# Gate products of the recurrent layer as one fp32 matmul on unsplit tiles, with a new transfer queue, smaller margins and scattered durations in the planner that sets the order

## The chip, the cores and the metric

The kernel runs on 1 core of one Trainium2 chip. The metric is the device time of one execution in microseconds (us). Three runs of the kernel before gave 1911.36, 1911.61 and 1918.54 us; their median is 1911.61 us. Engines are named as the profile names them: PE (matrix products), PEld (its weight loads), DVE, ACT, POOL, and SP, whose queue issues every transfer of this kernel.

## The reference

Two layers work on x, 2048 rows (frames) by 1024 columns. Each computes x = x + gate * Mixer(RMSNorm(x) * (1 + scale) + shift), where shift, scale and gate are one row each, a product of SiLU(c) with `ada_w`. A last RMSNorm follows. Everything is fp32.

```python
# layer 1: RG-LRU
proj = h @ in_w                                   # 1024 -> 2048: xb and zg
xf = causal_dwconv(xb, conv_w) + conv_b           # 4 taps
pre = einsum('bsni,knij->kbsnj', xf_by_block, gate_w) + gate_b   # 2 gates, 8 blocks of 128 x 128
r, i = sigmoid(pre)
log_a = -8 * r * softplus(-lam); a = exp(log_a)
b = sqrt(1 - exp(2 * log_a)) * (i * xf)
y = scan(h_t = a_t h_{t-1} + b_t) * silu(zg)
out = y @ out_w
# layer 2: gated DeltaNet, 8 heads of 128
q, k, v = silu(causal_dwconv(h @ in_w[:, :3072], conv_w)); z, a, b = the rest of h @ in_w
o = chunk_gated_delta_rule(l2norm(q), l2norm(k), v, decay(a), sigmoid(b))
out = (rmsnorm(o) * onorm_g * silu(z)) @ out_w
```

The product that the change rewrites is `pre`: for each of the 8 blocks of 128 columns, two 128x128 gate matrices times `xf`.

## The kernel before

**Tiles and stages.** The 2048 frames are cut into two halves u of 1024, each into two chunks i of 512. Activations lie with the columns on the partitions, so a tile is 128x512 fp32. Layer 1's input projection (`in1`) makes, for each u, n (0 to 7) and i, an x tile and a z tile; then the convolution, the gates and the scan follow in `conv1_thread` and `gates_thread`, and the result `tz` is stored to a DRAM tensor `y_d`. Layer 1's output projection (`out1_jobs`) goes through 16 blocks of 128 frames: `y_thread` loads a block from `y_d` into `yf` (one buffer, 512 KB), splits it into `yh` and `yl`, and two jobs multiply it with the weights. While it runs, the result goes to DRAM (`x_d`), comes back for the second layer's norm, is turned by 32x32 transposes that pass through DRAM (`xt_d<-xb`), and comes back as `xk` (`reload_thread`), of which `split_thread` makes the operands of layer 2's projection (`in2`). Layer 2's heads (keys, inverses, recurrence over 128-frame chunks) run between the products of `in2`; a z tile of layer 2 passes ACT (`zgate_thread`, L1042) and is stored to `z_d`. The last stage is layer 2's output projection.

**Split products.** The large products take both operands as two fp32r tiles, a rounded part and the rest, and add three products: high by high, high by low, low by high (`products`, L696; fp32r is a 4-byte type; the trace has one record for each such matmul). The gates did the same. This is the head of `gates_thread` before (L819 to L841), where `gh`, `gl` are the split gate weights that `lru_thread` makes once for each u and n (ACT `gh` L902, POOL `gl` L905):

```python
yield "act", 0.521
xh = tile_([P, TC], "xh", "xh", F32R)
act.copy(xh, xf)                                            # L828
yield "dve2", 0.599
xl = tile_([P, TC], "xr", "xl", F32R)
dve.tensor_tensor(xl, xf, f(xh), ALU.subtract)              # L831
for g in range(2):
    ctok = yield slots["c"]
    yield "pe", 0.696
    pg = ps.tile([P, TC], F32, tag="c", name="pg")
    for q, (a, b) in enumerate(((gh, xh), (gh, xl), (gl, xh))):
        pe.matmul(pg, lhsT=a[:, g, :], rhs=b, start=(q == 0), stop=(q == 2))   # L837
```

There are 2 x 8 x 2 = 32 such threads, so 64 gate products of three matmuls.

**What sets the order.** Every engine works through its instructions in the order in which they stand in the program, and one that waits holds back all behind it on that engine; SP's queue is one of these. The order is made before the run by `Weave`, a planner: each thread is a Python generator that yields what it needs next (an engine and a duration, a transfer, a buffer of a tag from `slots`, an event), and the planner keeps a clock for each engine and always lets the thread go on whose step can start first; the instruction is written there. So a number in a `yield` decides where an instruction stands, not how long it takes. `MARGIN` (2.4) is time that the planner adds behind certain transfers: all of it behind the loads of `vn` and `pq`, half of it before the cast of a layer 2 weight panel (`whi<-raw`), behind the load of `ec`, behind the stores of `hf` tiles, and behind some POOL steps. `transfer` says when the planner thinks that a transfer has landed:

```python
LANDS = {"sp": 1.375, "st": 1.07}        # loads, stores
self.free["sp"] = t + 0.45
self.free["dma"] = max(t + 1.04, self.free["dma"]) + dur
self.landed.append(self.free["dma"] + LANDS[kind])
th.t = self.landed[-1] + 0.05 if wait else t + 0.45
```

Of the kernel before, what the change touches and what calls it, by code (L numbers as in the profile page):

```python
# [9 lines left out]
F32R = mybir.dt.float32r  # L10
# [22 lines left out]
MARGIN = 2.4  # L33
# [5 lines left out]
WEIGHTS = 0.12  # L39
TABLE = 1.28  # L40
LANDS = {"sp": 1.375, "st": 1.07}
# [32 lines left out]
class Weave:  # L74
    def __init__(self):
        self.free = dict.fromkeys(("pe", "act", "dve", "pool", "sp", "dma"), 0.0)
        self.held = {"dve2": [], "pool2": []}
        self.table = "exp"
        self.landed = [0.0] * 8
        self.threads = []  # L80
        self.now = 0.0
# [19 lines left out]
    def start(self, th):  # L101
# [9 lines left out]
        if w[0] in LANDS:  # L111
            return max(th.t, self.free["sp"], self.landed[-8])
# [17 lines left out]
    def transfer(self, th, t, kind, dur, wait=True):  # L130

        self.free["sp"] = t + 0.45
        self.free["dma"] = max(t + 1.04, self.free["dma"]) + dur
        self.landed.append(self.free["dma"] + LANDS[kind])
        th.t = self.landed[-1] + 0.05 if wait else t + 0.45

    def run(self):
        while self.threads:
# [15 lines left out]
            elif w[0] in LANDS:  # L154
# [9 lines left out]
def trunk_kernel(ctx, tc, x, head, small, ada_w, ada_b, final_g, w1, gate_w, ow1, w2, wab, ow2, out):  # L164
# [64 lines left out]
    tags |= {t: ("l1", n) for t, n in {"xh": 2, "xf1": 2, "tg": 4, "th": 2, "tz": 2, "gw": 1, "gh": 1, "gl": 1, "head": 1}.items()}  # L229
# [79 lines left out]
    def first_loads_thread():  # L309

        yield ev("firstpanel")
        for half in range(2):
# [5 lines left out]
            for q in range(4):  # L318
                for n in (2 * half, 2 * half + 1):
                    part, d = FIRST[n]  # L320
                    yield "sp", 1.4, False
# [10 lines left out]
    def first_small_thread():  # L332
        yield "sp", 0.29, False
        sp.dma_start(out=head_s, in_=head)
        w.spawn(arrive_thread(ev("head")), 0)
        yield "sp", 0.29, False
# [82 lines left out]
    def row_halves_thread(parts):  # L419
# [3 lines left out]
        for layer, part, d in parts:  # L423
            ttok = yield slots["tt"]
            acc = tile_([P, TC], "tt", "acc")
            for q in range(4):
                wtok = yield slots["raw"]
                yield "sp", 1.4
# [27 lines left out]
            yield "sp", 1  # L456
# [6 lines left out]
            if layer == 1:  # L463
                yield "st", 0.29
# [60 lines left out]
    def turn_thread(key, t_d, xt, tok, ttok, b):  # L525
        yield from scale_thread(xt, ev("scaled", key, b), True)
        for d in range(2):
# [7 lines left out]
            for c_ in range(4):  # L535
                yield "st", 0.31, c_ == 3
# [86 lines left out]
    def panel_load(name, p):  # L623
# [3 lines left out]
        yield "sp", 1.4, False  # L627
# [5 lines left out]
    def panels_thread():  # L633
        yield ev("small")
        ahead = []
        for name, panels, _ in plans:
            for m, p in enumerate(panels):
# [23 lines left out]
                if name[1] > 0:  # L661

                    kept = yield ev("kept", p)
                    yield "sp", 1.4, False
# [18 lines left out]
    def keep_thread(p, lo):  # L683
        kept = dram.tile([P, KT, P], F32, name=f"wlo_d{p[0]}{p[1]}{p[2]}")
        yield "st", 1.4
# [133 lines left out]
    def gates_thread(u, n, i):  # L819
        xf, ftok = yield ev("xf", u, n, i)  # L820
        gh, gl = yield ev("gw", u, n)
        etok = yield slots["xh"]
        ltok = yield slots["xr"]
        if (u, n, i) == (NU - 1, KT - 1, NTC - 1):
            w.set(ev("lasthalves"))
        yield "act", 0.521
        xh = tile_([P, TC], "xh", "xh", F32R)
        act.copy(xh, xf)  # L828
        yield "dve2", 0.599
        xl = tile_([P, TC], "xr", "xl", F32R)  # L830
        dve.tensor_tensor(xl, xf, f(xh), ALU.subtract)  # L831
        for g in range(2):
            ctok = yield slots["c"]
            yield "pe", 0.696
            pg = ps.tile([P, TC], F32, tag="c", name="pg")
            for q, (a, b) in enumerate(((gh, xh), (gh, xl), (gl, xh))):
                pe.matmul(pg, lhsT=a[:, g, :], rhs=b, start=(q == 0), stop=(q == 2))  # L837
            w.spawn(gate_thread(u, n, i, g, pg, ctok), 3)
        put("xh", etok)
        put("xr", ltok)  # L840
# [36 lines left out]
        yield "st", 1  # L877
# [13 lines left out]
    def lru_thread():  # L891
        for u in range(NU):
            for n in range(KT):
                wtok = yield slots["gw"]
                yield "sp", 0.48
                gw = tile_([P, 2, P], "gw", "gw")
                sp.dma_start(out=gw, in_=gate_w[n])
                htok = yield slots["gh"]
                ltok = yield slots["gl"]
                yield "act", 0.302  # L900
                gh = tile_([P, 2, P], "gh", "gh", F32R)
                act.copy(gh, gw)  # L902
                yield "pool2", 1.02
                gl = tile_([P, 2, P], "gl", "gl", F32R)
                pool.tensor_tensor(gl, gw, f(gh), ALU.subtract)  # L905
                put("gw", wtok)
                w.set(ev("gw", u, n), (gh, gl))
# [4 lines left out]
                put("gh", htok)  # L912
                put("gl", ltok)


    def out_weights_thread(key, src, d, scale, slot, before, after):
# [5 lines left out]
        for k in range(0, KT, 2):  # L922
            rtok = yield slots["raw"]
            yield "sp", 1.4, False
# [18 lines left out]
    def y_thread():  # L943
        for b in range(S // P):
# [4 lines left out]
            yield "sp", 1.4  # L949
# [30 lines left out]
    def residual1_thread(b, d, pt, bank, mtok):  # L980
# [7 lines left out]
        yield "st", 1  # L988
# [4 lines left out]
    def xr_thread():  # L993
        yield ev("lasthalves")
        nb = S // P
        for b, d in [(b + q, d) for b in range(0, nb, 2) for d in range(2) for q in range(2)]:
            xtok = yield slots["xr"]
            yield "sp", 1
# [39 lines left out]
    def zgate_thread(u, h, i, pt, mtok, bank):  # L1038
# [5 lines left out]
        yield "st", 1  # L1044
# [4 lines left out]
    def decay_thread(u):  # L1049
        yield ev("tiles", (("in2", u), 0))  # L1050
        ttok = yield slots["tt"]
        yield "sp", 0.29
# [73 lines left out]
        yield "st", 0.29  # L1126
# [4 lines left out]
    def key_thread(u, h, i):  # L1131
# [4 lines left out]
        yield "sp", 1.2  # L1136
# [60 lines left out]
        for b in range(4):  # L1197
            yield "st", 0.078, b == 3
# [13 lines left out]
    def norm_q_thread(u, h, i):  # L1212
# [3 lines left out]
        yield "sp", 1.2  # L1216
# [18 lines left out]
    def tokens_of(ap, name):  # L1235
# [7 lines left out]
        for r in range(4):  # L1243
            yield "st", 0.31, r == 3
# [5 lines left out]
    def value_thread(u, h, i):  # L1250
# [5 lines left out]
        yield "sp", 1.2  # L1256
# [29 lines left out]
    def inverses_thread(u, h):  # L1286
# [6 lines left out]
        for g in range(4):  # L1293
            yield "sp", 0.59, g == 3
# [23 lines left out]
        for g in range(4):  # L1318
            yield "st", 0.15, g == 3
# [483 lines left out]
```

## Time and profile before

| | |
|---|---|
| median of three runs | 1911.61 us |
| the profiled execution's own time | 1915.63 us |
| its span, first to last instruction | 1913.9 us |
| mean granted TensorE clock | 0.988 |
| busy share PE, PEld, DVE, ACT, POOL | 96%, 78%, 71%, 62%, 20% |
| transfers | 322.77 MB in 510,427 packets |

A row of the page's groups reads: line, engine, operation, output <- inputs, shape, count | busy us, mean ns of one | idle time of the engine before them and what ended it. A timeline row has the start, the length, the engine and line, and in brackets the idle time before it and its releaser. Matmuls overlap: one record of 128x512 is about 0.39 us long, while they start about 0.23 us apart, so the pace is read from starts or from a run of many. A row of stages has the busy time of PE, PEld, DVE, ACT and POOL (with counts), then the granted clock, the busy share of the DMA engines and GB/s.

### The profile page before, as it was taken

What the parts mean: (1) busy time and instruction counts of PE and PEld (TensorE: products, weight loads), DVE (VectorE), ACT (ScalarE), POOL (GpSimd) and SP (SyncE); (2) the same over time, 40 slices, a digit from 0 to 9 for tenths busy, and PEclk for the clock granted to TensorE, in tenths of its full rate; (3) what the DMA queues carried; (4) which work ended last, traced back from release to release, by engine and by line L of the source; (5) the groups of instructions that cost most, each with busy time, mean ns of one, the idle gap of its engine ahead of it and who ended that gap; (6) DMA issues with size and microseconds to landing.
All of it is one profiled execution on the core that took longest, in us unless ns stands there. A gap on an engine that the chain in (4) does not pass through costs nothing.

```text
span 1913.9 us, 31154 instructions
## 1 busy us (share of the span) xinstructions
PE 1834.6 (96%) x10286; PEld 1492.7 (78%) x10286; DVE 1366.0 (71%) x3153; ACT 1183.9 (62%) x2749; POOL 382.1 (20%) x912
## 2 busy tenths in 40 slices
PE   6999898999999899999999999999999999999998
PEld 4777676888777678788788887787887877888887
DVE  7888977878644557768788876667676667767653
ACT  4666667777211348786787775677877668754221
POOL 1121210111000014133123321132232122211010
PEclk9999999999999899999999999999999999999999
DMA  8475736544688634557676667266554546587851
GB/s 345 123 219 156 239 121 205 170 160 158 220 207 217 207 92 143 152 134 182 162 183 179 145 149 216 73 164 153 123 149 117 148 129 155 138 219 220 252 154 67
DMA packets 510427, 322.77 MB, mean 169 GB/s; under 512 B 369844, under 2 KB 437940, under 8 KB 510264
## 3 DMA queue, kind: packets, MB, share of 16 engines
q1 hardware_dynamic: 510264, 320.77, 60.0%
q8 instruction: 81, 1.33, 0.3%
q14 instruction: 82, 0.67, 0.1%
HBM read 219.93 MB, written 100.73 MB: 168 GB/s over the span
## 4 chain that ended last, share of the span: by engine, by line
PE 35%; DVE 7%; DMA 6%; ACT 6%; SPq 3%; issue 2%; POOL 1%; DVEq 0%; POOLq 0%; ACTq 0%
PE mm L696 17%; PE mmo L696 9%; DVE xf L748 2%; DMA raw<-in_w 2%; PE py L1446 1%; PE pp L1429 1%; PE pS L1459 1%; PE pS L1458 1%; PE pp L1430 1%; SPq L1245 1%; DVE ttmp L1309 1%; DVE tblk L1312 1%; DMA oraw<-in_ow 1%; ACT junk L1163 1%; PE pkk L1186 1%
## 5 line engine op out<-in xcount | busy, mean ns | idle before, releaser
L748 DVE SCALAR_TENSOR_TENSOR xf<-xe,small_s,xf 128x512 f32<-128x512 f32 x288 | 214.6, 749 | 38.8 <-ACT xf L1027 34.2
L672 ACT CAST whi<-raw 128x1024 fp32r<-128x1024 f32 x96 | 100.2, 1044 | 47.8 <-DMA raw<-in_w 41.1
L1309 DVE TENSOR_TENSOR ttmp<-blk,tblk 128x60 f32<-128x60 f32 (+24 forms) x496 | 104.2, 210 | 29.6 <-DMA blk<-blk_d 6.6
L1312 DVE TENSOR_TENSOR tblk<-tblk,ttmp 128x60 f32<-128x60 f32 (+24 forms) x496 | 107.8, 217 | 12.1
L696 PE MATMUL mmo<-oh,yh 128*128 128x512 f32 x256 | 102.2, 399 | 8.0 <-ACT yh L955 8.0
L696 PE MATMUL mm<-hh_('in2', 0)_5289,whi 128*128 128x512 f32 x256 | 104.0, 406 | 4.5 <-ACT tz L1042 4.5
L696 PE MATMUL mm<-hh_('in2', 1)_12167,whi 128*128 128x512 f32 x256 | 104.3, 408 | 0.7 <-ACT xe L760 0.7
L696 PE MATMUL mm<-hh_('in2', 1)_11901,whi 128*128 128x512 f32 x256 | 105.0, 410 | 0.0
L696 PE MATMUL mm<-hl_('in2', 1)_12168,whi 128*128 128x512 f32 x256 | 104.7, 409 | 0.0
L696 PE MATMUL mm<-hh_('in2', 1)_12167,wlo 128*128 128x512 f32 x256 | 104.7, 409 | 0.0
L696 PE MATMUL mmo<-oh,yl 128*128 128x512 f32 x256 | 103.2, 403 | 1.4 <-DVE yl L959 1.3
L696 PE MATMUL mm<-hh_('in2', 1)_11901,wlo 128*128 128x512 f32 x256 | 104.0, 406 | 0.0
L696 PE MATMUL mm<-hl_('in2', 0)_5290,whi 128*128 128x512 f32 x256 | 103.7, 405 | 0.0
L696 PE MATMUL mm<-hh_('in2', 0)_5435,wlo 128*128 128x512 f32 x256 | 103.4, 404 | 0.0
L696 PE MATMUL mm<-hl_('in2', 1)_11902,whi 128*128 128x512 f32 x256 | 103.3, 403 | 0.0
L696 PE MATMUL mm<-hh_('in2', 0)_5289,wlo 128*128 128x512 f32 x256 | 103.1, 403 | 0.0
L696 PE MATMUL mmo<-oh,ol 128*128 128x512 f32 (+1 forms) x264 | 102.7, 389 | 0.0
L696 PE MATMUL mmo<-oh,oh 128*128 128x512 f32 (+1 forms) x264 | 102.7, 389 | 0.0
L696 PE MATMUL mm<-hh_('in2', 0)_5435,whi 128*128 128x512 f32 x256 | 102.5, 400 | 0.0
L696 PE MATMUL mmo<-ol,oh 128*128 128x512 f32 (+1 forms) x264 | 102.4, 388 | 0.0
L696 PE MATMUL mm<-hl_('in2', 0)_5436,whi 128*128 128x512 f32 x256 | 102.2, 399 | 0.0
L763 POOL COPY carry<-xe 128x4 f32<-128x4 f32 x96 | 23.7, 247 | 392.8 <-ACT xe L760 392.2
(322 smaller groups left out, 5549.6 us busy)
## 6 DMA issues: line engine op xcount, KB each, us to landing
raw<-in_w SPq DMA_DIRECT2D x96, 512.0 KB, 4.5
araw<-in_ada_w SPq DMA_DIRECT2D x32, 512.0 KB, 4.6
xt<-x_d SPq DMA_DIRECT2D x32, 512.0 KB, 5.3
xt_d<-xb SPq DMA_DIRECT2D x192, 64.0 KB, 2.4
xk<-xt_d SPq DMA_DIRECT2D x24, 512.0 KB, 6.4
xt<-in_x SPq DMA_DIRECT2D x16, 512.0 KB, 5.8
ada<-in_ada_w SPq DMA_DIRECT2D x16, 512.0 KB, 10.1
y_d<-tz SPq DMA_DIRECT2D x32, 256.0 KB, 3.5
```

The lines of the kernel that those rows point to most:

```text
L672: act.copy(hi, raw)
L696: pe.matmul(pt, lhsT=lhs[a][:, k, :], rhs=rhs[b][:, k, :], start=(k == 0 and n == 0), stop=(k == KT - 1 and n == 2))
L748: dve.scalar_tensor_tensor(xf, xe[:, 1 + j:1 + j + TC], wc[:, j:j + 1], xf, ALU.mult, ALU.add)
L763: pool.tensor_copy(out=carry, in_=xe[:, TC:TC + 4])
L1163: act.activation(junk, kd[:, b, :], AF.Square, accum_out=ss[:, b:b + 1])
L1186: pe.matmul(pkk[:, b, :], lhsT=kc, rhs=kc, start=True, stop=True)
L1245: sp.dma_start(out=dst[r], in_=tb[32 * r:32 * r + 32])
L1309: dve.tensor_tensor(tmp, blk[:, j, j + 1:32].unsqueeze(2).to_broadcast([P, r, c_]), t[:, j, 0:c_].unsqueeze(1).to_broadcast([P, r, c_]), A ...
L1312: dve.tensor_tensor(t[:, j + 1:32, 0:c_], t[:, j + 1:32, 0:c_], tmp, ALU.subtract)
L1429: pe.matmul(pp[:, 0, :], lhsT=kc, rhs=S_, start=True, stop=True)
L1430: pe.matmul(pp[:, 1, :], lhsT=qc, rhs=S_, start=True, stop=True)
L1446: pe.matmul(py, lhsT=rm[:, b, :], rhs=zt, start=True, stop=True)
```

## The change

It does three things.

- **Gates.** `xh`, `xl`, `gh` and `gl` are gone, and with them the ACT, DVE and POOL instructions that made them. Each gate product is one fp32 matmul of `gw` and `xf` as they are. The freed space gives `xf1` a third buffer and `gw` a second.
- **Planner.** Transfers go through a second, serial stage (`through`), with other constants for loads and stores, and nearly all sizes get new durations (a 64 KB store of a transposed tile 0.53 instead of 0.31, a 512 KB load 1.3 instead of 1.4, a `blk_d` store 0.13 instead of 0.078). `MARGIN` falls from 2.4 to 1.0.
- **Scatter.** Each planned duration of ACT, DVE and POOL is multiplied by 1 plus a normal deviate of 1%, drawn from a fixed seed.

The second and third change no instruction, only the order. By count PE loses 128 matmuls (192 gate matmuls become 64), DVE 32 instructions (`xl`), ACT 32 `xh` and 16 `gh` casts, POOL 16 `gl`; ACT gets 2 more table loads (119 to 121), and the transfers stay as many (1609 rows on SP).

```diff
-MARGIN = 2.4
+MARGIN = 1.0
+SEED, SPREAD = 58, 0.01
-LANDS = {"sp": 1.375, "st": 1.07}
+TRANSFER = {"sp": (1.56, 0.61, 0.05), "st": (0.74, 0.38, 0.5)}
...
     def engine(self, th, t, kind, dur, lag=None, table=None):
         e = th.last = kind.rstrip("2")
+        if e != "pe":
+            dur *= 1.0 + SPREAD * self.scatter.gauss(0.0, 1.0)
...
     def transfer(self, th, t, kind, dur, wait=True):
+        front, through, late = TRANSFER[kind]
         self.free["sp"] = t + 0.45
-        self.free["dma"] = max(t + 1.04, self.free["dma"]) + dur
-        self.landed.append(self.free["dma"] + LANDS[kind])
-        th.t = self.landed[-1] + 0.05 if wait else t + 0.45
+        self.free["dma"] = max(t + front, self.free["dma"]) + dur
+        self.through = max(self.free["dma"] + through, self.through + 0.22 + 0.38 * dur)
+        self.landed.append(self.through + 0.46)
+        th.t = self.landed[-1] + late if wait else t + 0.45
...
-    tags |= {t: ("l1", n) for t, n in {"xh": 2, "xf1": 2, "tg": 4, "th": 2, "tz": 2, "gw": 1, "gh": 1, "gl": 1, "head": 1}.items()}
+    tags |= {t: ("l1", n) for t, n in {"xf1": 3, "tg": 4, "th": 2, "tz": 2, "gw": 2, "head": 1}.items()}
...
-                yield "st", 0.31, c_ == 3
+                yield "st", 0.53, c_ == 3
                 sp.dma_start(out=dst[c_], in_=tb[32 * c_:32 * c_ + 32])
...
     def gates_thread(u, n, i):
         xf, ftok = yield ev("xf", u, n, i)
-        gh, gl = yield ev("gw", u, n)
-        etok = yield slots["xh"]
-        ltok = yield slots["xr"]
+        gw = yield ev("gw", u, n)
...
-        yield "act", 0.521
-        xh = tile_([P, TC], "xh", "xh", F32R)
-        act.copy(xh, xf)
-        yield "dve2", 0.599
-        xl = tile_([P, TC], "xr", "xl", F32R)
-        dve.tensor_tensor(xl, xf, f(xh), ALU.subtract)
         for g in range(2):
             ctok = yield slots["c"]
-            yield "pe", 0.696
+            yield "pe", 0.86
             pg = ps.tile([P, TC], F32, tag="c", name="pg")
-            for q, (a, b) in enumerate(((gh, xh), (gh, xl), (gl, xh))):
-                pe.matmul(pg, lhsT=a[:, g, :], rhs=b, start=(q == 0), stop=(q == 2))
+            pe.matmul(pg, lhsT=gw[:, g, :], rhs=xf, start=True, stop=True)
...
     def lru_thread():
...
-                act.copy(gh, gw)
...
-                pool.tensor_tensor(gl, gw, f(gh), ALU.subtract)
-                put("gw", wtok)
-                w.set(ev("gw", u, n), (gh, gl))
+                w.set(ev("gw", u, n), gw)
```

**Where instructions moved: PE, first gates.** PE's queue at the first gate products of layer 1 (`pg`), between the products of the second chunk's first panel (`mm`; `whi`, `wlo` are the split panel). Before, then after (lines below the head of the file stand 7 further down in the new file, up to the gates):

```order
L696 MATMUL mm<-hh_('in1', 0)_475,whi 128x512
L837 MATMUL pg<-xh,gh 128x512
L837 MATMUL pg<-xl,gh 128x512
L837 MATMUL pg<-xh,gl 128x512
L696 MATMUL mm<-hl_('in1', 0)_476,whi 128x512
L837 MATMUL pg<-xh,gh 128x512
L837 MATMUL pg<-xl,gh 128x512
L837 MATMUL pg<-xh,gl 128x512
L696 MATMUL mm<-hh_('in1', 0)_475,wlo 128x512
```
```order
L703 MATMUL mm<-hh_('in1', 0)_466,wlo 128x512
L835 MATMUL pg<-xf_453,gw 128x512
L703 MATMUL mm<-hh_('in1', 0)_466,whi 128x512
L835 MATMUL pg<-xf_453,gw 128x512
L703 MATMUL mm<-hl_('in1', 0)_467,whi 128x512
```

Each group of three became one, at nearly the same place among the panel's products, and no matmul is left that reads `xl`.

**SP, end of layer 1's output projection.** SP's queue around the load of the last block of `yf` (the last `yf` row in the program). Before, then after:

```order
L573 DMA xk<-xt_d 128x2x512 x3
L989 DMA x_d<-xr 128x512
L573 DMA xk<-xt_d 128x2x512
L951 DMA yf<-y_d 128x8x128
L573 DMA xk<-xt_d 128x2x512
L989 DMA x_d<-xr 128x512
L1000 DMA xr<-in_x 128x512
L573 DMA xk<-xt_d 128x2x512 x3
```
```order
L986 DMA xr<-in_x 128x512
L937 DMA yf<-y_d 128x8x128
L975 DMA x_d<-xr 128x512
L580 DMA xk<-xt_d 128x2x512 x4
L975 DMA x_d<-xr 128x512
L986 DMA xr<-in_x 128x512
L580 DMA xk<-xt_d 128x2x512 x3
L986 DMA xr<-in_x 128x512
L580 DMA xk<-xt_d 128x2x512
```

The last `yf` load stood behind four of the eight `xk` loads of 512 KB; now it stands ahead of all eight.

**SP, last z tiles of layer 2's first half.** SP's queue where the operands of the second half (`xk`) are loaded and two z tiles are stored (`z_d`). Before, then after:

```order
L686 DMA wlo_d2z_11591<-wlo 128x1024
L573 DMA xk<-xt_d 128x2x512 x3
L1045 DMA z_d<-tz 128x512 x2
L1218 DMA pq<-q_d 128x4x128
L629 DMA raw_11760<-in_w 128x1024
```
```order
L693 DMA wlo_d2z_11276<-wlo 128x1024
L1031 DMA z_d<-tz 128x512
L580 DMA xk<-xt_d 128x2x512 x3
L1031 DMA z_d<-tz 128x512
L1204 DMA pq<-q_d 128x4x128
```

Both stores stood behind three `xk` loads; now the first of them stands ahead of these.

More of the change, by code (lines that the diff above doesn't have):

```diff
@@ L1 @@
+import random
 from contextlib import ExitStack
@@ L78, in __init__ @@
         self.table = "exp"
-        self.landed = [0.0] * 8
+        self.landed, self.through = [0.0] * 8, 0.0
+        self.scatter = random.Random(SEED)
         self.threads = []
@@ L110, in start @@
         free = self.free.get(w[0].rstrip("2"), 0.0)
-        if w[0] in LANDS:
+        if w[0] in TRANSFER:
             return max(th.t, self.free["sp"], self.landed[-8])
@@ L153, in run @@
                 value, w.taken = w.taken, w.taken + 1
-            elif w[0] in LANDS:
+            elif w[0] in TRANSFER:
                 self.transfer(th, t, *w)
@@ L332, in first_small_thread @@
     def first_small_thread():
-        yield "sp", 0.29, False
+        yield "sp", 0.23, False
         sp.dma_start(out=head_s, in_=head)
         w.spawn(arrive_thread(ev("head")), 0)
-        yield "sp", 0.29, False
+        yield "sp", 0.23, False
         sp.dma_start(out=small_s, in_=small)
@@ L455, in row_halves_thread @@
                 n = 1
-            yield "sp", 1
+            yield "sp", 0.84
             j = 2 * part + d
@@ L626, in panel_load @@
         rtok = yield slots["raw"]
-        yield "sp", 1.4, False
+        yield "sp", 1.3, False
         raw = tile_([P, KT, P], "raw", f"raw{n}")
@@ L876, in gates_thread @@
         put("tg", itok)
-        yield "st", 1
+        yield "st", 1.1
         t0 = u * T + i * TC
@@ L948, in y_thread @@
             tok = yield slots["yf"]
-            yield "sp", 1.4
+            yield "sp", 1.3
             yf = tile_([P, KT, P], "yf", "yf")
@@ L987, in residual1_thread @@
         put(bank, mtok)
-        yield "st", 1
+        yield "st", 0.84
         sp.dma_start(out=x1_d[b * P:(b + 1) * P, d * TC:(d + 1) * TC], in_=xr)
@@ L997, in xr_thread @@
             xtok = yield slots["xr"]
-            yield "sp", 1
+            yield "sp", 0.84
             xr = tile_([P, TC], "xr", "xr")
@@ L1051, in decay_thread @@
         ttok = yield slots["tt"]
-        yield "sp", 0.29
+        yield "sp", 0.23
         wraw = tile_([P, KT, 16], "tt", "wabr")
@@ L1135, in key_thread @@
         etok = yield slots["ec"]
-        yield "sp", 1.2
+        yield "sp", 0.92
         ec = tile_([P, TB, P], "ec", "ec")
@@ L1197, in key_thread @@
         for b in range(4):
-            yield "st", 0.078, b == 3
+            yield "st", 0.13, b == 3
             q0 = b * NB + i * TB
@@ L1215, in norm_q_thread @@
         htok = yield slots["hf"]
-        yield "sp", 1.2
+        yield "sp", 0.92
         pq = tile_([P, TB, P], "hf", "pq")
@@ L1255, in value_thread @@
         ntk = yield slots["vn"]
-        yield "sp", 1.2
+        yield "sp", 0.92
         vn = tile_([P, TB, P], "vn", "vn")
@@ L1330, in levels_thread @@
             for b in range(4):
-                yield "sp", 0.078, i == NTC - 1 and b == 3
+                yield "sp", 0.016, i == NTC - 1 and b == 3
                 q0 = b * NB + i * TB
@@ L1570, in o_loads_thread @@
             tok = yield slots["b4"]
-            yield "sp", 1.4, False
+            yield "sp", 1.3, False
             on = tile_([P, KT, P], "b4", "on")
@@ L1574, in o_loads_thread @@
             ztok = yield slots["b4"]
-            yield "sp", 1.4, False
+            yield "sp", 1.3, False
             zs = tile_([P, KT, P], "b4", "zs")
@@ L1687, in rows_thread @@
         for name, src in (("g2", gate_d), ("fg", final_g)):
-            yield "sp", 1.4
+            yield "sp", 1.3
             row = tile_([P, D], name, name)
```

37 lines of the change are left out of this document (14 added, 23 removed).

## The prediction

> **What bounds the kernel now.** I read the page's busy shares first, then the stages, then what PE waited for in each, then the places of the longest waits.
>
> ```profile
> span 1913.9 us, 31154 instructions
> PE 1834.6 (96%) x10286; PEld 1492.7 (78%) x10286; DVE 1366.0 (71%) x3153; ACT 1183.9 (62%) x2749; POOL 382.1 (20%) x912
> ```
>
> PE is busy for 96% of the span. Its records overlap, so this alone does not prove that PE is the bound; the stages say where it had slack. The rows below are the start, layer 1's projection with its gates for the first half and some of the second, the rest of layer 1, its output projection, layer 2, and the last projection; the columns are PE, PEld, DVE, ACT, POOL, granted clock, DMA share, GB/s.
>
> ```profile
> 0.00:60.00 60.00, 44.40 (x182) 29.59 (x182) 46.09 (x108) 28.13 (x46) 11.49 (x30) 0.97 0.70 276
> 60.00:345.00 285.00, 264.93 (x1124) 212.69 (x1124) 239.16 (x391) 190.50 (x278) 48.64 (x65) 0.98 0.61 185
> 345.00:490.00 145.00, 144.63 (x639) 117.83 (x638) 119.59 (x200) 106.95 (x146) 23.67 (x29) 1.00 0.53 168
> 490.00:690.00 200.00, 189.47 (x798) 148.59 (x797) 101.79 (x151) 43.40 (x57) 8.69 (x25) 0.97 0.68 192
> 690.00:1758.00 1068.00, 1042.44 (x6879) 861.49 (x6878) 776.90 (x2210) 779.00 (x2147) 273.32 (x718) 1.00 0.61 155
> 1758.00:1914.00 156.00, 148.75 (x671) 122.51 (x669) 82.42 (x96) 35.91 (x78) 16.29 (x46) 0.98 0.52 160
> ```
>
> From 345 to 490 us PE has 0.4 us of idle time: work added there is paid in full. From 60 to 345 us it stands still for 20 us while DVE is busy 239 of 285 us (84%), so there PE and DVE take turns as the bound. From 490 to 690 us PE loses 10.5 us, in layer 2 (690 to 1758 us) 25.6 us. What ended these waits, for PE, in the second, fourth and fifth stage (us in total, times, longest):
>
> ```profile
> PE mm L696 <- DVE xf L786: 10.0, 6, 3.2
> PE pg L837 <- DVE xl L831: 5.1, 3, 4.4
> PE mm L696 <- DVE tz L815: 3.8, 2, 2.0
> PE mmo L696 <- ACT yh L955: 8.0, 3, 6.3
> PE mm L696 <- ACT tz L1042: 4.5, 2, 3.8
> PE py L1446 <- DVE zt L1438: 2.5, 5, 0.8
> ```
>
> In layer 1 PE waits for DVE alone; afterwards two single waits, 6.3 and 3.8 us, make a good part of the loss. The rest of layer 2's waits are under 2.5 us in total for each pair, over many places.
>
> **The gates' price on PE.** The costs are read from these rows: the three gate matmuls, the parts that go (`xl`, `xh`, `gh`, `gl`), and two runs of one kind on PE: eight fp32 records of 128x512 (`adaps`, products of the conditioning vector) and, from the chain that ended last, 33 fp32r ones.
>
> ```profile
> L837 PE MATMUL pg<-xl,gh 128*128 128x512 f32 x64 | 26.5, 414 | 5.1 <-DVE xl L831 5.1
> L831 DVE TENSOR_TENSOR xl<-xf,xh 128x512 fp32r<-128x512 f32 x32 | 23.3, 736 | 3.8 <-ACT xh L828 3.4
> L828 ACT CAST xh<-xf 128x512 fp32r<-128x512 f32 x32 | 19.8, 618 | 46.6 <-DVE xf L799 46.3
> L905 POOL TENSOR_TENSOR gl<-gw,gh 128x256 fp32r<-128x256 f32 x16 | 14.6, 915 | 50.4 <-ACT gh L902 50.4
> L902 ACT CAST gh<-gw 128x256 fp32r<-128x256 f32 x16 | 6.5, 404 | 0.8 <-DMA gw<-in_gate_w 0.8
> 20.45 3.60 PE L365 MATMUL adaps<-ada,c_bc 128*128 128x512 f32 x8
> 1121.47 7.53 PE mm L696 x33
> 19.59 0.59 PE L365 MATMUL adaps<-ada,c_bc 128*128 128x512 f32 x1
> ```
>
> The program has 16 `adaps` matmuls and the trace 32 records, so an fp32 matmul is two records. Eight last 3.60 us, the last of them 0.59: (3.60 - 0.59) / 7 = 0.430 us from start to start, 0.86 us for a product. An fp32r matmul of that shape takes 7.53 / 33 = 0.228 us, three 0.684 us. Each gate product thus costs 0.86 - 0.684 = 0.176 us more, and 64 cost +11.2 us. This is PE work in stages where PE is the bound or nearly so: all of it goes on the path. The Trainium skill, "FP8 and Floating Point Precision", section TensorE Precision Notes, has true fp32 as four passes through the array; at 0.228 us a pass that would be 0.91 us a product and +14.6 us in all, 3.4 us more than the rows give. The trace's pace decides here.
>
> **What the gates give back.** POOL's 14.6 us and ACT's 26.3 us bring nothing by themselves: POOL is 20% busy, ACT 67% in the second stage, and none of the PE waits quoted for that stage names either. DVE's 23.3 us count, since DVE is what PE waits for there. One chain of waits falls for certain:
>
> ```profile
> 228.33 0.39 PE L837 MATMUL pg<-xh,gh 128*128 128x512 f32 x1
> 233.10 0.79 PE L837 MATMUL pg<-xl,gh 128*128 128x512 f32 x1 [4.38 <-DVE xl L831]
> 237.38 0.80 PE L696 MATMUL mm<-hh_('in1', 0)_226,whi 128*128 128x512 f32 x1 [1.78 <-DVE tz L815]
> 239.25 0.63 PE L696 MATMUL mm<-hl_('in1', 0)_227,whi 128*128 128x512 f32 x1
> 230.00:242.00 12.00, 7.12 (x16) 5.16 (x17) 10.77 (x20) 9.28 (x14) 5.83 (x2) 0.63 0.72 246
> ```
>
> PE stood 4.38 us for `xl`, then 1.78 us for a `tz`, which on DVE stands behind the two `xl` of this place. After the first wait the matmuls are 0.63 us long instead of 0.39, and the granted clock from 230 to 242 us is 0.63: 0.37 x 12 = 4.4 us lost, some 0.9 of it inside the second wait. With no `xl` there is nothing to wait for here: -(4.4 + 1.8 + 3.5) = -9.7 us. The other DVE waits (10.0 + 5.1 + 3.8 less the 6.2 just counted, 12.7 us) come from a DVE at 84%; without `xl` (two thirds of 23.3 us, 15.5) it has 223.7 of 285 us, 78%. I take 8 of the 12.7 us away; the ends are 0 and 12.7. A third `xf1` and a second `gw` buffer cost nothing: no PE wait above names them.
>
> **The order at the end of layer 1.** The last `yf` load stands behind four `xk` loads, SP's own rows and what ACT and PE did:
>
> ```profile
> 636.01 1.46 SPq L573 DMA_DIRECT2D xk<-xt_d  x3
> 638.57 0.41 SPq L951 DMA_DIRECT2D yf<-y_d  x1
> 649.33 1.03 ACT L955 CAST yh<-yf 128x1024 fp32r<-128x1024 f32 x1
> 650.41 0.80 PE L696 MATMUL mmo<-oh,yh 128*128 128x512 f32 x1 [6.29 <-ACT yh L955]
> 650.40:656.50 6.10, 5.88 (x13) 4.18 (x14) 3.72 (x6) 2.20 (x3) 0.00 (x0) 0.52 0.80 276
> yf<-y_d SPq DMA_DIRECT2D x16, 512.0 KB, 4.7
> ```
>
> The cast begins 10.8 us after the load was issued, where a `yf` load takes 4.7 us in the median. PE waits 6.29 us and then runs at a clock of 0.52 for 6.1 us, which costs 0.48 x 6.1 = 2.9 us. In the changed order the load stands ahead of all eight `xk` loads, and ACT's cast ahead of all of their `h` tiles: at 4.7 us it lands some 6 us earlier, and the wait and the clock loss go: -9.2 us. The ends are 0, if the transfers already under way hold it up as much, and -9.2. Late next are the `xk` loads, by one 512 KB load; they are wanted only when the last `mmo` products are through.
>
> **The order of the z stores.** The 3.8 us wait in layer 2:
>
> ```profile
> 1146.36 1.88 SPq L573 DMA_DIRECT2D xk<-xt_d  x3
> 1148.34 0.89 SPq L1045 DMA_DIRECT2D z_d<-tz  x2
> 1156.30 0.60 ACT L1042 ACTIVATE tz<-mm 128x512 f32<-128x512 f32 x1 [4.99 <-DMA z_d<-tz]
> 1156.95 0.50 PE L696 MATMUL mm<-hh_('in2', 0)_5289,whi 128*128 128x512 f32 x1 [3.79 <-ACT tz L1042]
> 1156.00:1162.00 6.00, 5.05 (x21) 3.66 (x22) 1.18 (x6) 0.60 (x1) 0.00 (x0) 0.72 0.87 269
> ```
>
> ACT had no free `tt` tile until the first z store, behind three `xk` loads, had landed 8 us after its issue. PE lost 3.8 us and 0.28 x 6 = 1.7 us by the clock. The store now goes ahead of the loads: I take 4.5 of the 5.5 us, ends 0 and 5.5.
>
> **The smaller margins.** They are the part that can cost. Layer 2's panel casts were planned 1.04 + 1.4 + 1.375 + 0.05 + 1.2 = 5.07 us after the load's issue, and are now 1.56 + 1.3 + 0.61 + 0.46 + 0.05 + 0.5 = 4.48 us (the generator's constants, with the queue empty). What the load takes, and how ACT fared with the old margin in layer 2:
>
> ```profile
> raw<-in_w SPq DMA_DIRECT2D x96, 512.0 KB, 4.5
> ACT whi L672 <- DMA raw<-in_w: 20.9, 18, 3.4
> ```
>
> The median load fitted by 0.6 us and now just fits, so about half of layer 2's 64 casts come late by up to 0.6 us more: 32 x 0.6 = 19 us more waiting in ACT's queue, at the most 64 x 0.6 = 38. ACT is busy 779 of 1068 us there, so most is idle time moved. Today 20.9 us of such waits go with 25.6 us of PE idle time of every cause, so little of them can reach PE: I take +3 us of the 19, ends 0 and +38. The 1% scatter changes which of two near equal steps stands first; its mean is zero, and I price it by a third of layer 2's waits, +-8 us.
>
> **The sum.** +11.2 - 9.7 - 8 - 9.2 - 4.5 + 3 = -17.2 us. The profiled execution took 1915.63 us (span 1913.9 and 1.7 around it), so 1898.4 for such a one; it is 4.0 us (0.2%) above the median of the runs, 1911.61, and from that the forecast is 1894 us, 0.9% faster.
>
> **Rivals.** (1) *The order gives more.* The planner's serial transfer stage removes waits of the same kind that I did not look for. With all ends of the terms above (+11.2 - 9.7 - 12.7 - 9.2 - 5.5) and half of the remaining 20 us of layer 2's waits: -36, 1876 us. For it speaks that both moved places follow from one cause; against it, that layer 2's other waits name DVE and ACT chains, not transfers.
>
> (2) *The gates' cost is not given back.* DVE, at 78%, makes PE wait at other places, and only the `xl` wait itself goes: +11.2 - 9.7 + 0 - 9.2 - 4.5 + 3 + 4 (scatter) = -5, 1906 us. For it speaks the stage from 345 to 490 us, where nothing can be given back.
>
> (3) *The moved transfers land as late as before.* The transfers ahead of `yf` include turned 64 KB stores, and the DMA engines are 80% busy from 650 us. Then -17.2 + 9.2 + 4.5 = -3.5, 1908 us. The Trainium skill, "DMA: Bandwidth & Descriptors", section Queues, rings and completion order, says that completions are not first in, first out for an issuing engine, so a load issued later need not land later, and this rival would follow. The row speaks against it: 10.8 us for the load behind four others, 4.7 us in the median.
>
> (4) *Slower: the margins turn into waits of ACT.* In layer 2 ACT, in order, holds up PSUM copies behind each late cast. It decides once over 17.2 + 9.6 - 3 = 24 us more of the 38 reach PE: then 1921 us or more. Against it stands that ACT is 73% busy, and that the largest PE wait on ACT there (4.5 us, `tz`) comes from a store, not from a panel.
>
> **How the numbers follow.** The likeliest case, the terms about as taken (1884 to 1904), has 0.47; rival 1, below 1884, 0.20; rival 2 0.13 and rival 3 0.08, 1904 to 1915; rival 4 and a bad draw of the scatter, above 1915, 0.12. No change is 1902 to 1921 us (0.5%, about what such runs can tell). Faster: 0.20, and 0.43 of the likeliest case, with 0.02 from rivals 2 and 3: 0.65. Slower: 0.10. Same: 0.25. The range goes down to rival 1's bound with some of the scatter, 1870, and up to the edge where rival 4 begins, 1920, which leaves out about 0.05 and 0.11.
>
> **What would show it.** Right: 128 `pg` records from 64 products at 0.43 us from start to start; no `xl`, and PE's waits on DVE between 60 and 345 us at 5 us or less; no wait over 2 us for `yh` or `tz`, and two stretches of half clock fewer; PE's loss in layer 2 within 8 us of 25.6. Wrong: PE's waits on `xf` and `tz` as long as before (rival 2), `yf` again landing after 8 us (rival 3), or ACT's waits for `raw` over 50 us with PE's loss in layer 2 above 40 us (rival 4).

## The result, and the profile after

The changed kernel takes 1881.89 us in the median of six runs (1876.22 to 1886.06); the kernel before takes 1911.68 us in six runs beside it. The ratio is 0.9833 with a 95% interval of 0.9812 to 0.9853: 29.8 us or 1.7% faster. Forecast were 1894 us and 17.6 us, so the direction and the range held, and the gain was 12 us larger than the sum.

The profiled execution of after took 1877.61 us, 4.3 us under its median; that of before took 1915.63, 4.0 us over its own. The two traces therefore differ by 38.0 us where the medians differ by 29.8. Trace numbers below add up to 38, and some 8 us of that is spread between executions.

The header and busy shares of the page of after:

```profile
span 1875.9 us, 30928 instructions
PE 1831.7 (98%) x10222; PEld 1472.3 (78%) x10222; DVE 1347.0 (72%) x3121; ACT 1163.4 (62%) x2703; POOL 359.6 (19%) x896
```

PE is busy as long as before (1834.6 us), though the gates cost more there. So the gain is idle time and clock of PE, not PE work. The same stages as shown of before, with the same columns (PE, PEld, DVE, ACT, POOL, granted clock, DMA share, GB/s):

```profile
60.00:345.00 285.00, 280.40 (x1152) 213.63 (x1151) 246.16 (x409) 194.09 (x270) 42.42 (x60) 1.00 0.66 201
345.00:490.00 145.00, 144.62 (x594) 110.77 (x593) 104.44 (x166) 85.39 (x112) 15.67 (x20) 1.00 0.51 167
490.00:690.00 200.00, 197.34 (x868) 158.19 (x868) 106.13 (x173) 56.71 (x83) 11.28 (x32) 1.00 0.65 186
690.00:1758.00 1068.00, 1053.76 (x6926) 868.68 (x6925) 783.95 (x2195) 775.25 (x2144) 268.77 (x721) 1.00 0.62 160
```

From 60 to 345 us PE's idle time fell from 20.1 to 4.6 us and the clock rose from 0.98 to 1.00; in layer 2 idle time fell from 25.6 to 14.2. These windows are fixed in time while the work moved forward, so I use five stages cut at the same events in both traces: the start, the last product of `in1`, the first of `in2`, the first of `in2`'s second half, the last of `in2`, and the end.

| stage | before, us | after, us | difference |
|---|---|---|---|
| start and layer 1's projection | 473.7 | 461.5 | -12.2 |
| layer 1's output projection | 196.3 | 179.2 | -17.1 |
| layer 2, first half | 516.4 | 514.2 | -2.2 |
| layer 2, second half | 529.1 | 518.9 | -10.2 |
| the rest | 198.4 | 202.1 | +3.7 |

The rest has 984 PE records after and 952 before, and 2 us more of idle time: a part of the last work (32 small `px` matmuls) that stood ahead of the cut now stands behind it. The cut between layer 2's halves is not quite clean either: before, 16 products for the second half (`pab`, 3.7 us at 0.23 us each) stood ahead of it, and now they stand behind.

### The profile page after: what moved, and what is told of

The parts are those of the page before. It is cut to its first block, busy times and chain, and to the rows that moved or that the text cites. A ratio compares the mean times of both kernels' runs of the same rounds, so it can differ in the third digit from the quotient of the medians.

```text
span 1875.9 us, 30928 instructions
## 1 busy us (share of the span) xinstructions
PE 1831.7 (98%) x10222; PEld 1472.3 (78%) x10222; DVE 1347.0 (72%) x3121; ACT 1163.4 (62%) x2703; POOL 359.6 (19%) x896
## 4 chain that ended last, share of the span: by engine, by line
PE 75%; DVE 7%; DMA 6%; ACT 6%; issue 2%; SPq 2%; POOL 2%; DVEq 0%; POOLq 0%; ACTq 0%
PE mm L703 40%; PE mmo L703 18%; DMA raw<-in_w 3%; PE pg L835 3%; DMA oraw<-in_ow 2%; PE py L1432 1%; PE pp L1415 1%; PE pS L1445 1%; PE pS L1444 1%; PE pqk L1260 1%; PE pp L1416 1%; PE adaps L372 1%; PE pkk L1172 1%; PE pab L1058 1%; DVE xf L755 1%
## 5 line engine op out<-in xcount | busy, mean ns | idle before, releaser
L1298 DVE TENSOR_TENSOR tblk<-tblk,ttmp 128x60 f32<-128x60 f32 (+24 forms) x496 | 106.3, 214 | 12.4
L703 PE MATMUL mm<-hh_('in2', 0)_4993,whi 128*128 128x512 f32 x256 | 105.2, 411 | 0.0
L703 PE MATMUL mm<-hh_('in2', 1)_11807,wlo 128*128 128x512 f32 x256 | 104.8, 409 | 0.0
L703 PE MATMUL mm<-hl_('in2', 1)_11604,whi 128*128 128x512 f32 x256 | 104.7, 409 | 0.0
L703 PE MATMUL mm<-hh_('in2', 1)_11603,wlo 128*128 128x512 f32 x256 | 104.7, 409 | 0.0
L703 PE MATMUL mm<-hh_('in2', 0)_4993,wlo 128*128 128x512 f32 x256 | 104.4, 408 | 0.0
L703 PE MATMUL mm<-hh_('in2', 1)_11603,whi 128*128 128x512 f32 x256 | 104.2, 407 | 0.0
L703 PE MATMUL mm<-hl_('in2', 0)_4994,whi 128*128 128x512 f32 x256 | 103.8, 406 | 0.0
L703 PE MATMUL mm<-hl_('in2', 1)_11808,whi 128*128 128x512 f32 x256 | 103.8, 405 | 0.0
L703 PE MATMUL mm<-hh_('in2', 1)_11807,whi 128*128 128x512 f32 x256 | 103.8, 405 | 0.0
L703 PE MATMUL mm<-hh_('in2', 0)_5108,wlo 128*128 128x512 f32 x256 | 103.5, 404 | 0.0
## 6 DMA issues: line engine op xcount, KB each, us to landing
ada<-in_ada_w SPq DMA_DIRECT2D x16, 512.0 KB, 10.2
```

What stands on the lines that cost most here:

```text
L703: pe.matmul(pt, lhsT=lhs[a][:, k, :], rhs=rhs[b][:, k, :], start=(k == 0 and n == 0), stop=(k == KT - 1 and n == 2))
L1298: dve.tensor_tensor(t[:, j + 1:32, 0:c_], t[:, j + 1:32, 0:c_], tmp, ALU.subtract)
```

## The experiments

Each ratio is to the kernel before, run beside it on the same chip, with its 95% interval; where one execution was taken, its time is given alone.

**Gates alone.** The kernel before with its old planner, constants and durations; only the gate products are rewritten.

```diff
...
-    for q, (a, b) in enumerate(((gh, xh), (gh, xl), (gl, xh))):
-        pe.matmul(pg, lhsT=a[:, g, :], rhs=b, start=(q == 0), stop=(q == 2))
+    pe.matmul(pg, lhsT=gw[:, g, :], rhs=xf, start=True, stop=True)
...
```

> The kernel before with the gate part alone: one fp32 matmul for each gate product, no xh, xl, gh, gl, three xf1 and two gw buffers; MARGIN, transfer model and durations as before, no scatter. Theory A (most of the gain of 30 us is the planner's transfers and margins, and layer 1's gates give 5 to 8 us): 1903 to 1907 us, layer 1's projection 4 to 9 us shorter, layer 2 as before. In this order the last yf load also happens to stand ahead of all xk loads, so by A the 9 us of that wait go too: 1895 to 1899. Theory B (most of the gain is the relief of DVE in layer 1, the planner brings little): 1880 to 1888.

Measured: 0.9928 (0.9903 to 0.9953), 1896.48 us. A gain of 12.8 us, less than half of the whole, and where theory A had it. The gates do relieve layer 1: its projection ends at 459.9 us instead of 473.7, and PE, busy for 264.93 of 285 us in this stage before, hardly stands still now:

```profile
60.00:345.00 285.00, 282.56 (x1152) 215.18 (x1151) 241.77 (x403) 205.87 (x279) 37.49 (x60) 0.99 0.64 197
```

Not all of this is the gates' own work. With fewer instructions the old planner also makes another order: the last `yf` load stands ahead of the `xk` loads, and the output projection takes 184.8 us for 196.3, while layer 2 takes 1050.4 for 1045.5.

**Planner alone.** The new planner, constants, durations and scatter with the old split gates.

```diff
-MARGIN = 2.4
+MARGIN = 1.0
+SEED, SPREAD = 58, 0.01
...
-LANDS = {"sp": 1.375, "st": 1.07}
+TRANSFER = {"sp": (1.56, 0.61, 0.05), "st": (0.74, 0.38, 0.5)}
...
```

> The changed kernel with the split gates of before (three fp32r matmuls, xh, xl, gh, gl): planner, margin, durations and scatter as changed. Theory A: 1886 to 1892 us, with PE's waits in layer 1's projection near the 20 us of before. Theory B: 1902 to 1912. The last yf load stands ahead of all xk loads here too.

Measured: 0.9849 (0.9823 to 0.9875), 1880.64 us. This is the whole change within the intervals (0.9833, 0.9812 to 0.9853), and faster than theory A had it: with the new order the gate edit adds nothing that can be told. Alone the two parts gain 0.7% and 1.5%, together 1.7%, so in part they remove the same waits: each shortens layer 1's projection (by 13.8 and 7.8 us), and each moves the last `yf` load ahead (output projection 184.8 and 181.3 us). PE's row from 60 to 345 us with the new order and split gates, and what PE waited for there (it stands still for 14.3 us, where I had expected near 20):

```profile
60.00:345.00 285.00, 270.66 (x1158) 218.43 (x1158) 247.29 (x406) 200.72 (x290) 52.55 (x67) 0.97 0.63 192
```
```profile
PE mm L703 <- ACT whi L679: 10.7, 2, 7.8
PE mm L703 <- DVE wlo L685: 2.0, 2, 1.3
PE pg L844 <- DVE xl L838: 1.2, 1, 1.2
```

The wait for `xl`, 5.1 us before, is 1.2 us here without the gate edit. Two late panel casts took its place, so layer 1's projection ends at 465.9 us, and at 461.5 with the gates too.

**No scatter.** The changed kernel with `SPREAD = 0.0`.

> The changed kernel with SPREAD 0: the planned durations are not scattered. Theory A: within 8 us of the changed kernel, 1874 to 1890, on either side. Theory C (the seed was a lucky draw and carries a third or more of the gain): 1892 or more.

Measured: 0.9865 (0.9839 to 0.9892), 1885.22 us. The gain is there without the scatter.

**The old margin.** The changed kernel without scatter and with `MARGIN = 2.4`.

> The changed kernel with SPREAD 0 and MARGIN 2.4 as before: against the run without scatter it tells what the smaller margin is worth under the new transfer model. If shorter margins cost ACT waits (my term of +3 us on PE), this is 0 to 5 us faster than that run, with fewer ACT waits on raw loads; if they bring something by freeing buffers earlier, it is 5 to 12 us slower, in layer 2.

Measured: 0.9878 (0.9856 to 0.99), 1886.62 us, 1.4 us over the run without scatter, where I had expected 0 to 5 us under it. The margins are worth nothing that can be told, either way. ACT's waits for panels in layer 2, first without scatter at the margin of 1.0, then at 2.4:

```profile
ACT whi L679 <- DMA raw<-in_w: 26.7, 21, 4.7
```
```profile
ACT whi L679 <- DMA raw<-in_w: 21.1, 15, 3.9
```

The smaller margin costs ACT 5.6 us of waiting over 1068 us, and no PE wait of layer 2 names `whi` in either trace.

**Two other draws of the scatter.** The changed kernel with `SEED = 1` and with `SEED = 2`.

> The changed kernel with seed 1 in place of 58. Theory A: 1874 to 1890 us. Theory C (the seed carries a third or more of the gain): 1890 to 1900, and the stage that differs is layer 2.

> The changed kernel with seed 2 in place of 58; the same expectations as with seed 1: theory A 1874 to 1890, theory C 1890 to 1900. The spread of the three seeds is the price of the scatter, for which I took 8 us.

Measured: 0.9852 (0.9821 to 0.9882) and 0.9881 (0.9851 to 0.991). The four draws that were run (seed 58, none, 1, 2) give 0.9833, 0.9865, 0.9852 and 0.9881, a spread of 0.5%. The one in the change is the lowest of the four, but the intervals of the first three overlap, and every draw keeps more than two thirds of the gain: theory A, with seed 2 at the edge of its range. Where they differ is layer 2, in their profiled executions (us; before as in the table of stages):

| | before | seed 58 | no scatter | seed 1 | seed 2 |
|---|---|---|---|---|---|
| layer 1 with its output projection | 670.0 | 640.7 | 638.3 | 637.6 | 639.6 |
| layer 2, first half | 516.4 | 514.2 | 515.7 | 513.4 | 526.4 |
| layer 2, second half | 529.1 | 518.9 | 525.7 | 531.0 | 521.7 |

Layer 1 is some 30 us shorter with every draw. Layer 2 is 12.4 us shorter with seed 58, 4.1 and 1.1 without scatter and with seed 1, and 2.6 longer with seed 2.

**Old transfers and durations, small margin.** The gates alone with `MARGIN = 1.0`.

> The fp32 gates and MARGIN 1.0, but the transfer model and the durations of before and no scatter. Here the last yf load stands behind three xk loads. Theory A (the transfer model is what orders transfers well): 1895 to 1908 us, with a wait of PE for yh of 4 us or more near the end of layer 1's output projection and ACT's waits for raw loads above 20.9 us in layer 2. If the margin alone is what helps: 1880 to 1888.

Measured: 0.9945 (0.9926 to 0.9965), 1901.51 us. The margin does not bring the gain either. The time is theory A's, and ACT's waits for raw loads are 33.5 us in layer 2; but PE's wait of 4 us or more for `yh` did not come. The last `yf` load stands behind five `xk` loads here, not three as I had counted, and PE's waits for `yh` in the whole output projection are 2.8 us, the longest 1.3:

```profile
610.20 0.94 SPq L573 DMA_DIRECT2D xk<-xt_d  x2
611.70 5.64 SPq L573 DMA_DIRECT2D xk<-xt_d  x3
619.40 0.37 SPq L930 DMA_DIRECT2D yf<-y_d  x1
625.05 1.03 ACT L934 CAST yh<-yf 128x1024 fp32r<-128x1024 f32 x1
```
```profile
PE mmo L696 <- ACT yh L934: 2.8, 3, 1.3
```

The five loads were issued over some 7 us, and the cast began 5.7 us after the issue of the `yf` load. In the kernel before, four loads were issued within 2.5 us right ahead of it, and it took 10.8. So the number of loads ahead is not the price by itself. Left for the gain are the serial stage and the durations.

**New durations with the old transfer rule, and the reverse.** Both have the new gates and `MARGIN = 1.0`, no scatter. The first keeps the old rule with its constants and takes all new durations; the second takes the serial stage with its constants and keeps the old durations. Both edits are shown against the changed kernel.

```diff
 # new durations, old rule
-        front, through, late = TRANSFER[kind]
...
-        self.free["dma"] = max(t + front, self.free["dma"]) + dur
-        self.through = max(self.free["dma"] + through, self.through + 0.22 + 0.38 * dur)
-        self.landed.append(self.through + 0.46)
-        th.t = self.landed[-1] + late if wait else t + 0.45
+        self.free["dma"] = max(t + 1.04, self.free["dma"]) + dur
+        self.landed.append(self.free["dma"] + {"sp": 1.375, "st": 1.07}[kind])
+        th.t = self.landed[-1] + 0.05 if wait else t + 0.45
 # serial stage, old durations
-                yield "st", 0.53, c_ == 3
+                yield "st", 0.31, c_ == 3
...
```

> fp32 gates, MARGIN 1.0, no scatter, all durations as changed, but transfers reckoned by the rule of before (no second stage, the old constants). The last yf load stands behind two xk loads. Between the run with old transfers and old durations (1901.5 us) and the one with both new (1885.2). If the durations carry the gain (a turned 64 KB store planned at 0.53 instead of 0.31): 1883 to 1890, the stage of layer 1's output projection near 179 us. If the second stage and its constants carry it: 1896 to 1903, that stage at 185 us or more.

> fp32 gates, MARGIN 1.0, no scatter, transfers by the new rule with its second stage and constants, but all durations as before. The last yf load stands ahead of all xk loads. If the second stage carries the gain: 1883 to 1890 us, layer 1's output projection near 179 us; if the durations do: 1896 to 1903, 185 us or more.

Measured: 1887.21 and 1897.97 us, in both the range of the durations. With the runs above they make a square (new gates, margin 1.0, no scatter in all four):

| | old durations | new durations |
|---|---|---|
| old transfer rule | 0.9945 (0.9926 to 0.9965) | 0.9856 (0.9833 to 0.9879) |
| serial stage | 0.9921 (0.9905 to 0.9937) | 0.9865 (0.9839 to 0.9892) |

The durations are worth 0.9% under the old rule and 0.6% under the new one, with intervals apart in both rows. The serial stage is worth -0.2% and +0.1%, with intervals that overlap. With the new gates it is the planner's table of durations, not its new queue, that carries what the planner adds. Each cell is one order, and draws of one table differ by up to 0.5%, so the share is known to that only. All the orders with new gates agree, though: the six with new durations have 0.9833 to 0.9881, the three with old ones (gates alone, and the left column) 0.9921 to 0.9945. Which of the many durations does it was not tried, nor the square with the split gates. It lies in layer 2 (us of both halves in the profiled execution; 1045.5 before):

| | old durations | new durations |
|---|---|---|
| old transfer rule | 1054.9 | 1042.4 |
| serial stage | 1055.2 | 1041.4 |

The durations take 12.5 and 13.8 us off layer 2. But of that nine to ten us only win back what layer 2 loses with the new gates under the old durations; the kernel before had 1045.5. The kernel with the serial stage alone does have the short output projection (179.7 us, as I had expected only if the second stage carried the gain), but loses in layer 2's first half (531.7 us):

```profile
640.00:1170.00 530.00, 514.02 (x3221) 422.06 (x3220) 394.88 (x1094) 377.02 (x1028) 132.43 (x357) 0.97 0.59 153
```

That is 16 us of idle PE time and, at a clock of 0.97, as much again (0.03 x 530).

**The gate products doubled.** In the changed kernel each gate product is computed twice in a row.

```diff
     pe.matmul(pg, lhsT=gw[:, g, :], rhs=xf, start=True, stop=True)
+    pe.matmul(pg, lhsT=gw[:, g, :], rhs=xf, start=True, stop=True)
```

> The changed kernel with every gate matmul issued twice into the same bank (the second one overwrites the first), with the order otherwise as it is: 64 more fp32 products of 128x512. If a product costs the 0.86 us of the adaps rows and all of it is on the path: +55 us on layer 1's projection. If it costs four passes of 0.228 (0.91): +58. If slack hides a part: under +45.

Measured: 1927.52 us in one execution, 49.9 us over the profiled execution of after. From the start of the first product to that of its double it takes 0.857 us in the median, 54.8 us for all 64. They lengthen layer 1's projection by 48.7 us; the first product of `in2` is 50.6 us later. So about nine tenths of PE work added to the gates arrives. Of the rest 3.3 us fill idle time of PE in that stage (16.6 us of it are left of 19.9). How full PE then is, in a window widened by that work (1.2 of 314 us idle):

```profile
60.00:374.00 314.00, 312.76 (x1222) 227.38 (x1221) 242.91 (x402) 194.53 (x268) 42.96 (x60) 1.00 0.60 180
```

**The last `yf` load moved, both ways.** In the kernel before, the first `xk` loads of `in2` are held until the last `yf` load is issued; in the changed kernel that load is held until four of the eight `xk` loads are issued.

```diff
 # before, yf first
     def reload_thread(key, t_d):
+        if key == (("in2", 0), 0):
+            yield ev("yflast")
...
+            if b == S // P - 1:
+                w.set(ev("yflast"))
 # after, yf behind
             tok = yield slots["yf"]
+            if b == S // P - 1:
+                yield ev("loaded", (("in2", 0), 0))
```

> The kernel before with one edit: the xk loads for layer 2's first chunk are not planned before the last yf load, which so stands ahead of all of them. My term: PE's 6.3 us wait for yh at the end of layer 1's output projection and the half clock behind it go, 9 us of that stage (196 us from the first product of that projection to the first of layer 2's, so some 187). If the transfers under way hold the load up as much (rival 3): no shorter than 194.

> The changed kernel with one edit: the last yf load waits until the first four xk loads are issued, as it stood before. My term: PE waits 4 to 7 us for yh again at the end of layer 1's output projection, with a half clock behind it, and that stage (179 us in the changed kernel) grows by 6 to 10 us. Rival 3: under 2 us.

One execution each: 1905.93 us, and 1881.64 us. At the place itself the two mirror each other: the output projection shrinks from 196.3 to 184.6 us (-11.8) in the one and grows from 179.2 to 189.6 (+10.4) in the other, a little more than my term in both. In the changed kernel with the load behind, SP's and ACT's rows of the timeline:

```profile
616.41 2.38 SPq L580 DMA_DIRECT2D xk<-xt_d  x4
618.89 0.83 SPq L939 DMA_DIRECT2D yf<-y_d  x1
627.72 0.81 ACT L595 ACTIVATE h<-xk,cond 128x512 f32<-128x512 f32 x1 [0.24 <-DVE hl_('in2', 0)_4992 L605]
628.44 1.03 ACT L943 CAST yh<-yf 128x1024 fp32r<-128x1024 f32 x1
```

PE's wait for that cast (total, times, longest), and its row from then to the end of the projection:

```profile
PE mmo L703 <- ACT yh L943: 5.9, 1, 5.9
```
```profile
629.50:639.80 10.30, 9.60 (x27) 7.14 (x28) 3.68 (x7) 2.31 (x3) 0.00 (x0) 0.62 0.52 189
```

The time from issue to landing of its 16 `yf` loads, of which this one is the longest:

```profile
DMA to landing us min/median/max: 3.8/4.9/7.6
```

The wait of 5.9 us and the low clock after it (0.38 x 10.3 = 3.9 us) are back: 9.8 of the 10.4 us. The load itself landed 7.6 us after its issue, at 626.5 us; the cast began 1.9 us later, since ACT was then in a row of `h` tiles that the same `xk` loads had released. So the place costs by two mechanisms, the transfer and ACT's queue. At the end of the program 3.3 us of the 10.4 are left (span 1879.2 for 1875.9): layer 2's two halves came out 2.8 and 3.1 us shorter. In the other trial 9.7 of the 11.8 us are there at the end (span 1904.2 for 1913.9), with layer 1's projection 3.1 us shorter though PE's order in it is the same, and layer 2 5.1 us longer. All orders behind the moved step are another draw, and with one execution each, and 3 us between two executions of one order in one stage, these trials show what the place costs and not how much of it arrives.

## Why the prediction was right or wrong, step by step

**The gates' price, forecast +11.2: right.** The group of after has 128 records from 64 products, as forecast:

```profile
L835 PE MATMUL pg<-xf,gw 128*128 128x512 f32 x128 | 66.0, 597 | 3.4 <-DVE xf L806 3.0 <-ACT tg L883 0.4
```

Three rows of its timeline, where a gate product (two records) stands between products of the panel:

```profile
110.82 1.02 PE L835 MATMUL pg<-xf,gw 128*128 128x512 f32 x2
111.28 0.79 PE L703 MATMUL mm<-hh_('in1', 0)_226,whi 128*128 128x512 f32 x1
111.91 0.39 PE L703 MATMUL mm<-hl_('in1', 0)_227,whi 128*128 128x512 f32 x1
```

From 110.82 to 111.91 one gate product and one of the panel pass: 1.09 us, less 0.23 for the latter is 0.86. Over all places with panel products around them the median is 0.87 us, against 0.69 us for the three matmuls before: 64 x 0.18 = 11.5 us. The Trainium skill, "FP8 and Floating Point Precision", section TensorE Precision Notes, has true fp32 as four passes, which at the pace of an fp32r matmul here is an estimate of 0.91 us and +14.6 us in all. The trace shows less.

**What layer 1 gives back, forecast -17.7 (net -6.5): under-sized; measured net -12.2.** The DVE waits went nearly whole (4.2 us are left, under the 5 that I had named). What is left of PE's waits from 60 to 345 us:

```profile
PE pg L835 <- DVE xf L806: 2.7, 2, 1.5
PE mm L703 <- DVE wlo L685: 1.5, 1, 1.5
PE pg L835 <- ACT tg L883: 0.4, 1, 0.4
```

From 60 to 345 us idle time fell by 15.5 us and the clock rose by 0.02 (5.7 us): 21.2, where I had 17.7. The clock had been priced at one wait alone. The cause was half right. The gates do it under the old planner (-13.8 us net alone), but the new planner takes 7.8 us off the same stage without them, and I had put all of it down to the gates. Rival 2, that the cost is not given back, is out.

**The `yf` order, forecast -9.2: right as a term, under-sized as a stage.** The moved load is worth -11.8 and +10.4 us in the two trials. The stage gained 17.1. Its row before and after, and the timeline of after at the load:

```profile
473.90:670.00 196.10, 185.57 (x777) 147.75 (x776) 109.80 (x162) 48.66 (x61) 10.55 (x23) 0.97 0.75 213
```
```profile
461.70:640.50 178.80, 178.42 (x773) 144.70 (x772) 98.64 (x143) 45.14 (x56) 9.57 (x22) 1.00 0.74 215
```
```profile
615.48 0.38 SPq L937 DMA_DIRECT2D yf<-y_d  x1
617.19 3.72 SPq L580 DMA_DIRECT2D xk<-xt_d  x4
621.15 1.05 ACT L941 CAST yh<-yf 128x1024 fp32r<-128x1024 f32 x1 [6.96 <-DMA yf<-y_d]
```

Idle time fell from 10.5 to 0.4 us, and the clock gave some 6 us (0.03 x 196 = 5.9). The sum held one wait of 6.3 us and 2.9 us of clock; the smaller waits for `yh` and `yl` in this stage (1.7 and 1.3 us) and the rest of the clock went too. The load was issued at 615.48 and the cast began 5.7 us later instead of 10.8; rival 3, as late as before, is out. Rival 1 was wrong, though, to put the moved places down to one cause, the serial stage: with the gates alone and the old planner the load stands ahead of the `xk` loads as well, and that stage takes 184.8 us.

**The z stores, forecast -4.5: the wait went, the gain did not stay.** No PE wait on `tz` is left in layer 2. But its first half, where that wait had been, is only 2.2 us shorter, less than the 3.7 us of `pab` products that left it. PE's idle time there is 12.3 us for 13.2; these waits took the place of the old one:

```profile
PE pgc L1090 <- DVE gg L1085: 2.7, 1, 2.7
PE px L1366 <- DVE ac L1360: 2.3, 1, 2.3
PE pqk L1260 <- ACT qt L1020: 1.7, 3, 1.0
```

**The margins, forecast +3, ends 0 and +38: nothing.** ACT's row in layer 2, 20.9 us before, is after:

```profile
ACT whi L679 <- DMA raw<-in_w: 28.2, 22, 6.5
```

ACT's added waiting is 7 us in the whole change, 5.6 by the margin alone, and not 19, and no PE wait in layer 2 names these casts. Rival 4 is out by a wide distance. The working started from the median load and the planner's constants; that half the casts would be late by 0.6 us was the weak step. Rival 4's bound has a slip as well: the sum held 3 us of margins already, so it needs 17.2 + 9.6 + 3 = 30 of the 38 us, not 24.

**What the sum did not hold: layer 2's second half, -10.2 us, much of it this draw.** PE's rows there, before and after:

```profile
1186.40:1715.50 529.10, 517.74 (x3467) 428.41 (x3466) 363.02 (x1085) 390.15 (x1091) 133.37 (x358) 0.99 0.56 142
```
```profile
1154.90:1673.80 518.90, 517.41 (x3453) 426.60 (x3452) 365.28 (x1085) 390.94 (x1094) 131.72 (x359) 1.00 0.56 146
```

As much PE work (517.4 us busy for 517.7) with 1.5 us of idle time in place of 11.4. PE had waited there on eleven different DVE and ACT chains, none for more than 2.2 us in total; one is left, of 1.2 us. I had forecast PE's loss in the window of layer 2 within 8 us of 25.6, and it is 14.2: of my signs of being right the one that failed. The size of the gain lies near rival 1 (1876 us), and it goes by another mechanism than I gave it: I had further waits on transfers go, by the serial stage, and what went are waits on DVE and ACT chains. The square has the durations as what shortens layer 2, which my working took as a detail of the transfer model. But against the kernel before, the other draws of the same durations give layer 2 4.1 and 1.1 us less and 2.6 us more, where seed 58 gives 12.4 less. So what all draws keep is layer 1's 30 us; most of layer 2's gain over the kernel before looks like luck of the draw, as far as one profiled execution of each shows. The planner alone, with seed 58 and split gates, has 1029.6 us in layer 2, but no other seed was run with it, and no run shows why these orders fall well.

**The scatter, +-8 us: right for the total, too small for a stage.** Four draws lie within 8.0 us in the median. Layer 2's halves differ more: over these draws the first takes 513.4 to 526.4 us and the second 518.9 to 531.0.

## What to carry to other kernels

Where a planner sets the order, a faster instruction and a better order may remove the same waits: cost each against the other, not both against the old trace. New durations in the planner's table can be worth more than a finer rule for queues, and their gain comes as many small waits that no single row of the old profile announces. So can a lucky draw: run more than one order of a planner before a gain in a stage is put down to a cause. A single moved load is priced well from its own rows, but what follows it is another draw.

## What the runs showed of the hardware

The granted clock followed waits more widely than I had priced: over the whole output projection it was 0.97 before and 1.00 after, so that some 6 of the stage's 17.1 us were clock and not idle time. In the trace of before, the clock was 0.50 for 10.2 us at the waits of 4.4 and 6.3 us (from 233.1 and 646.1 us), and for 3.4 us after the wait of 3.8 us. It was 0.50 for 3.4 us from 598.3 us too, where PE had waited 1.5 and 0.5 us, while behind a wait of 3.2 us (ended at 197.3 us) it stayed at 1.00: the length of a wait alone did not decide it here.

PE work added to a stage that PE fills arrives nearly whole: 54.8 us of added gate products in layer 1 became 49.9 at the end. And a second fp32 product on the same operands, straight behind the first, costs 0.857 us, where one among other matmuls costs 0.86 to 0.87: next to nothing of the first is saved.
